# Low parts of split weights by an accumulating transfer: a two-layer hybrid encoder on one core

## The chip, the cores and the metric

One core of a Trainium2 chip runs the kernel. The metric is the device time of one execution in microseconds (us). The engines are TensorE (PE in the profile; its weight loads are PEld), VectorE (DVE), ScalarE (ACT), GpSimd (POOL), and SyncE (SP), which here issues all transfers.

## The reference

Two layers, each on 512 tokens of 1024 channels: an RMS norm modulated by a conditioning vector, one large input projection `w_in`, three branches, and an output projection.

```python
for l in range(DEPTH):
    mod = c_act @ w_ada[l] + b_ada[l]
    shift, scale, gate = jnp.split(mod, 3, axis=-1)
    h = rms_norm(x, norm_w[l]) * (1.0 + scale[:, None, :]) + shift[:, None, :]
    proj = h @ w_in[l]
    ya = mixer_a(qa, ka, va, ...) * jax.nn.silu(ga)
    yb = mixer_b(qb, kb, vb, ...) * jax.nn.silu(gb)
    yc = mixer_c(xc, zc, bc, cc, dtf, dtb, ...)
    g_a, g_b, g_c = jnp.split(jax.nn.sigmoid(mg + b_gate[l]), N_BRANCH, axis=-1)
    merged = (g_a * (ya @ w_proj_a[l]) + g_b * (yb @ w_proj_b[l])
              + g_c * (yc @ w_proj_c[l]))
    x = x + gate[:, None, :] * (merged @ w_out[l])
```

Branch A is grouped-query attention, branch B banded attention at three dilations, branch C a state-space scan in both directions. All of it is in float32.

## The kernel before

**Split matmuls.** TensorE is given its operands as float32r, a rounded float32. Each operand is therefore written as a high part (the value rounded to float32r) and a low part (what the rounding lost), and a product is the sum of three matmuls: high weight by high activation, high weight by low activation, low weight by high activation.

**Chunks.** The weights are stored as 84 chunks per layer of 128 x 1024 numbers (512 KB), each with eight blocks of 128 x 128. `chunk` (line 478) makes one ready: SP loads it into a tile `wraw`, ACT copies it into `whi` with the rounding, and DVE subtracts: `wlo = wraw - whi`. `mm` (line 500) then runs over the blocks k, and for each block `mm_k` (line 490) issues the three matmuls, 24 per chunk, all into one PSUM bank. `proj` (line 510) does this for one 128-channel piece of the input projection; `branch_steps` (line 1217) for the projections of the branches; `out` (line 1247) for the output projection. `v_pair` (line 818) has its own order of the three products. At the start of a layer a few chunks use tiles named `u4` instead of `whi` and `wlo` and are multiplied by `mm_k` directly (lines 1299 to 1303 and 1318 to 1333). Of the 168 chunks, 158 use the tag `wlo`.

**Slots.** Every tile belongs to a tag, and a tag has a fixed number of slots (`SLOTS`, line 408): three each of `wraw`, `whi` and `wlo`. Tiles of 32 conditioning weights (`ada`, line 637) also use `wraw`, and the first sixteen use `whi` and `wlo`.

**Order.** Nothing is issued as written. `Rec.record` (line 199) notes each operation with its cost by a model (a transfer costs its issuing queue 520 or 650 ns, and its bytes divided by a rate on the transfer engines), and `Rec.schedule` (line 277) plans all of them: whichever engine is free takes the ready operation with the lowest priority number for which slots are free. A chunk's preparation is moved ahead of its place by `AHEAD` = 1114 operations (line 415). The plan fixes the order on each engine's queue; on the chip each queue runs in that order and waits where it must. For some operations the plan chooses the engine (`either` and `any2`): the scaling of probabilities and the products and masks of mixer C go to DVE, POOL or ACT.

**Stages of a layer.** Mixer A, mixer B with the projections of branch A, mixer C with those of branch B, then branch C and the output projection. In mixer C, `ssd_head` (line 1162) runs scans on DVE (tiles `P`), multiplies them on POOL or DVE into `u` tiles, ACT copies the high part of each, POOL or DVE makes the low part, and PE multiplies them into `ps_pv`. Gates and projections of other branches fill PE meanwhile.

In the profile nearly all instructions have line 404, where the planned operations are issued, so rows are told apart by their tiles.

Of the kernel before, what the change touches and what calls it, by code (L numbers as in the profile page):

```python
# [7 lines left out]
F32 = mybir.dt.float32  # L8
F32R = mybir.dt.float32r
I32 = mybir.dt.int32  # L10
AF = mybir.ActivationFunctionType
ALU = mybir.AluOpType
# [119 lines left out]
def cost_pe(name, kw, args):  # L132
    if name == "transpose":
        return max(56, 0.417 * args[1].p * 2 + 2, 0.83 * args[1].n)
    l, r = kw["lhsT"], kw["rhs"]
    if r.dt == F32:
        return 2 * max(0.833 * r.n + 2, 0.833 * l.n, 25)
    return max(0.417 * r.n + 2.5, 0.833 * l.n, 25)


def cost_dve(name, out, ins, ptr, n):
    ps = any(v.t.psum for v in ins) or out.t.psum
    if name == "reciprocal":
        return 69 + 6.25 * n
    if name == "tensor_tensor_scan":
        return 69 + SCAN * n
    if name == "memset":
        return 40 + 0.5 * n
    two = len([v for v in ins if v.n and v.n > 1 and v.n >= n]) > 1
    if not two and not ps and name != "tensor_reduce":  # L150
        return 69 + 0.52 * n + 61 * ptr
    return 69 + 1.042 * n + 61 * ptr


def cost_act(name, out, ins, ptr, acc, n):
    return (52 if ins and ins[0].t.psum else 94) + 0.833 * n + 93 * bool(ptr) + 93 * acc


def cost_pool(name, out, ins, ptr, n):
    if name in ("tensor_scalar",):  # L160
        return 245 + 0.83 * n
    if name == "memset":
        return 100 + 0.4 * n
    return 148 + (2.1 if all(v.n == n and not v.wide for v in ins) else 1.67) * n
# [15 lines left out]
class Rec:  # L180
# [18 lines left out]
    def record(self, alts):  # L199
        op = Op()  # L200
        op.i = len(self.ops)
        op.prio = op.i + self.boost
        op.alts = {}
        op.dma = 0
        op.urgent = self.urgent and alts[0][1] != "dma_start"
        for eng, meth, args, kw in alts:
            kw = dict(kw)
            if meth == "matmul":
                kw["lhsT"], kw["rhs"] = args[1], args[2]
            out = kw.get("out", args[0] if args else None)  # L210
            writes = [out] if isinstance(out, V) else []
            if isinstance(kw.get("accum_out"), V):
                writes.append(kw["accum_out"])
            reads = [a for a in args[1:] if isinstance(a, V)] + \
                    [v for k, v in kw.items() if isinstance(v, V) and k not in ("out", "accum_out")]
            n = out.n if isinstance(out, V) else 1
            ptr = sum(1 for v in reads if v.n == 1 and n > 1)
            if meth == "dma_start":
                v = out if isinstance(out, V) else reads[0]
                op.dma = v.n * v.p * 4  # L220
                c = 520
            elif eng == "tensor":
                c = cost_pe(meth, kw, args)
            elif eng == "vector":
                if meth == "tensor_reduce":
                    n = reads[0].n
                c = cost_dve(meth, out, reads, ptr, n)
            elif eng == "scalar":
                c = cost_act(meth, out, reads, ptr, "accum_out" in kw, n)
            else:  # L230
                c = cost_pool(meth, out, reads, ptr, n)
            if meth == "matmul":
                kw.pop("lhsT"), kw.pop("rhs")
            op.alts[ENG[eng]] = (c, eng, meth, args, kw)
        deps = {}
        pe = eng == "tensor"
        for v in reads:
            for o, box, w in v.t.log:
                if w and self.meet(box, v.box):
                    deps[o] = LAT  # L240
        for v in writes:
            if pe and v.t.psum and v.t.lastpe is not None:
                deps.setdefault(v.t.lastpe, 0)
            for o, box, w in v.t.log:
                if o is not op and self.meet(box, v.box) and not (pe and "PE" in o.alts):
                    deps[o] = LAT
        for v in writes:
            if pe and v.t.psum:
                v.t.lastpe = op
            v.t.log = [e for e in v.t.log if not self.inside(e[1], v.box)] + [(op, v.box, True)]  # L250
        for v in reads:
            v.t.log.append((op, v.box, False))
        op.tiles = list({id(v.t): v.t for v in reads + writes}.values())
        for t in op.tiles:
            if t.left == 0:
                t.seq = len(self.tags.setdefault(t.tag, []))
                self.tags[t.tag].append(t)
            t.left += 1
        deps.pop(op, None)
        if meth == "dma_start" and self.hold is not None:  # L260
            deps.setdefault(self.hold, -2000)
        if op.dma and self.hold is not None:
            op.alts = {e: (650,) + a[1:] for e, a in op.alts.items()}
        op.deps = deps
        op.succ = []
        self.ops.append(op)
        return op
# [137 lines left out]


class Kernel:
    SLOTS = {"wraw": 3, "whi": 3, "wlo": 3, "h": 16, "xs": 7, "gate": 3, "merged": 8, "tmp": 6, "P": 3, "bias": 1, "u4": 12, "q": 4, "s1": 32, "sm": 8, "dt": 2, "wa": 1}
    RESERVE = {"u4": 5, "tmp": 2, "sm": 3, "s1": 9, "ps_mm": 0, "ps_tp": 0, "wraw": 0, "q": 1, "ps_pv": 3}
    BYTES = {"wraw": 4096, "whi": 4096, "wlo": 4096, "u4": 4096, "P": 3072, "bias": 10240, "s1": 32, "sm": 256, "dt": 256,  # L410
             "dtr": 256, "dt96": 384}
# [13 lines left out]
    def __init__(self, nc, tc, A, depth=DEPTH, dbg=None):  # L425
        self.real_nc, self.tc, self.A, self.depth, self.dbg = nc, tc, A, depth, dbg or {}
        slots = dict(self.SLOTS)
        slots.update({"ps_" + k: n for k, n in self.BANKS.items()})
# [49 lines left out]
    def chunk(self, l, j, tags=("wraw", "whi", "wlo"), ahead=None, pool=False):  # L478
        nc = self.nc
        b, self.rec.boost = self.rec.boost, self.rec.boost - (self.AHEAD if ahead is None else ahead)  # L480
        raw = self.t(tags[0], [128, 1024])
        nc.sync.dma_start(raw, self.A["wch"][l, j])
        hi = self.t(tags[1], [128, 1024], F32R)
        nc.scalar.copy(hi, raw)
        lo = self.t(tags[2], [128, 1024], F32R)
        self.sub(lo, raw, hi.bitcast(F32), pool)
        self.rec.boost = b
        return hi, lo

# [8 lines left out]
        nc.tensor.matmul(ps, lo[:, c], xh, start=False, stop=(k == nk - 1), **kw)  # L498

    def mm(self, ps, w, c0, nk, xs):  # L500
        for k in range(nk):
            self.mm_k(ps, w, c0, k, nk, xs)

    def soon(self, f):

# [1006 lines left out]
```

## Time and profile before

| | |
|---|---|
| median of 3 runs | 1316.05 us (1314.54 to 1318.47) |
| profiled execution | 1322.19 us |
| its span, first to last instruction | 1320.4 us |
| mean granted TensorE clock | 0.991 |
| instructions | 17528 |
| moved by DMA | 144.30 MB |

The span is what rows and shares of the trace refer to; 1.8 us of the execution lie around it. Busy time of an engine doesn't count issuing and waiting. A wait in a row is idle time of an engine just before an instruction, named with what ended it. Matmuls overlap, so the busy time of a matmul is longer than its distance to the next.

### The profile page before, as it was taken

The page shows a single profiled execution, that of the slowest core. Times are in us where ns is not written, and L with a number is a line of the kernel's source. Part 1 is how long each engine was busy: PE and PEld are TensorE (multiplying, and loading weights), DVE is VectorE, ACT ScalarE, POOL GpSimd, SP SyncE. Part 2 cuts the span into 40 slices and gives each one's busy share as a digit, 9 for nine tenths or more (in the row PEclk, how much of TensorE's full clock was granted, in tenths as well). Part 3 has the DMA queues.
Part 4 walks back from the last instruction along what each step waited for, and adds up shares of the span by engine and source line. Part 5 has one row for each costly group of instructions (what it writes and reads, how often), then busy time and mean ns, then how long its engine had stood idle before and what let it go on. Part 6 is the DMA issues. An engine that isn't in the chain of part 4 may idle for free.

```text
span 1320.4 us, 17528 instructions
## 1 busy us (share of the span) xinstructions
PE 1234.5 (93%) x6240; PEld 1002.4 (76%) x6240; DVE 1040.2 (79%) x1798; ACT 667.4 (51%) x1132; POOL 373.3 (28%) x322
## 2 busy tenths in 40 slices
PE   4899999989999888999999999999998988989998
PEld 1678888778777667778888788887876866767887
DVE  7979975978799989974675999476598998998642
ACT  4447764666555445333334477556565443543330
POOL 3321220011035759610111222100002268583100
PEclk9999999999999999999999999999999999999999
DMA  7644214545322222234632421253342221222441
GB/s 283 237 122 121 69 47 154 187 140 178 108 59 78 64 64 64 66 110 144 222 129 63 130 96 50 79 183 89 95 132 56 81 64 55 73 64 80 136 137 63
DMA packets 49429, 144.30 MB, mean 109 GB/s; under 512 B 7350, under 2 KB 10038, under 8 KB 49342
## 3 DMA queue, kind: packets, MB, share of 16 engines
q1 hardware_dynamic: 49342, 143.19, 34.9%
q8 instruction: 49, 0.80, 0.3%
q14 instruction: 38, 0.31, 0.1%
HBM read 124.74 MB, written 4.27 MB: 98 GB/s over the span
## 4 chain that ended last, share of the span: by engine, by line
PE 63%; DVE 19%; POOL 7%; ACT 4%; issue 3%; DMA 3%; SPq 1%; DVEq 0%; POOLq 0%; ACTq 0%
PE ps_mm L404 47%; PE ps_sc L404 6%; PE ps_tp L404 6%; PE ps_pv L404 5%; DVE P L404 3%; DVE u L404 3%; POOL u L404 3%; DVE wlo L404 3%; DVE xs L404 2%; POOL P L404 1%; DVE q L404 1%; ACT u L404 1%; POOL bias L404 1%; DVE tmp L404 1%; ACT tmp L404 1%
## 5 line engine op out<-in xcount | busy, mean ns | idle before, releaser
L404 PE MATMUL ps_mm<-h,whi 128*128 128x512 f32 x1840 | 601.4, 397 | 1.8 <-ACT gate L404 1.5
L404 PEld LDWEIGHTS ps_mm<-h,whi 128*128 128x128 f32 x1840 | 345.3, 190 | 77.9 <-ACT gate L404 4.8
L404 PE MATMUL ps_mm<-h,wlo 128*128 128x512 f32 x920 | 364.6, 396 | 0.0
L404 DVE TENSOR_TENSOR wlo<-wraw,whi 128x1024 fp32r<-128x1024 f32 x158 | 208.4, 1321 | 84.6 <-ACT whi L404 83.2
L404 ACT CAST whi<-wraw 128x1024 fp32r<-128x1024 f32 x158 | 165.6, 1049 | 179.6 <-PE ps_mm L404 161.1
L404 PEld LDWEIGHTS ps_mm<-h,wlo 128*128 128x128 f32 x920 | 174.4, 190 | 34.7
L404 PE MATMUL ps_mm<-u,whi 128*128 128x512 f32 (+1 forms) x592 | 172.7, 374 | 0.0
L404 POOL TENSOR_SCALAR P<-P,s 128x512 f32<-128x512 f32 (+1 forms) x63 | 54.9, 873 | 339.3 <-DVE s L404 236.0
L404 PE MATMUL ps_pv<-u,u 128*128 128x256 f32 (+2 forms) x640 | 107.0, 293 | 28.4 <-ACT u L404 15.0
L404 PEld LDWEIGHTS ps_mm<-u,whi 128*128 128x128 f32 x592 | 107.7, 188 | 20.0 <-DVE gate L404 0.6
L404 PEld LDWEIGHTS ps_pv<-u,u 128*128 128x128 f32 (+1 forms) x640 | 81.3, 173 | 48.8 <-ACT u L404 21.2
L404 PE MATMUL ps_mm<-u,wlo 128*128 128x512 f32 (+1 forms) x296 | 110.0, 373 | 0.0
L404 ACT CAST u<-ps_tp 128x512 fp32r<-128x512 f32 (+2 forms) x174 | 71.8, 428 | 57.0 <-PE ps_tp L404 47.6
L404 DVE TENSOR_TENSOR_SCAN P<-ps_sc,bias 128x128 f32<-128x128 f32 (+3 forms) x128 | 98.7, 803 | 0.1
L404 DVE TENSOR_TENSOR u<-ps_tp,u 128x512 fp32r<-128x512 f32 (+2 forms) x174 | 81.9, 487 | 19.6 <-ACT u L404 18.9
L404 PE MATMUL ps_sc<-u,q 128*128 128x256 f32 (+1 forms) x320 | 85.9, 365 | 5.5 <-DMA u<-u 3.5
L404 POOL TENSOR_TENSOR tmp<-tmp,tmp 128x512 fp32r<-128x512 f32 (+1 forms) x22 | 32.4, 1474 | 180.4 <-ACT tmp L404 177.4
L404 POOL TENSOR_TENSOR u<-P,u 128x384 f32<-128x384 f32 (+3 forms) x68 | 69.3, 1030 | 15.0 <-DVE P L404 11.4
L404 PE MATMUL ps_tp<-const,P 128*128 128x128 f32 x448 | 67.6, 273 | 5.6 <-DVE s L404 2.3
L404 PEld LDWEIGHTS ps_tp<-const,P 128*128 128x128 f32 x448 | 53.7, 140 | 19.8 <-issue 7.2
L404 PEld LDWEIGHTS ps_sc<-u,q 128*128 128x128 f32 x320 | 52.9, 191 | 19.8 <-issue 6.5
L404 POOL TENSOR_TENSOR u<-u,u 128x1024 fp32r<-128x1024 f32 x24 | 62.3, 2595 | 12.8 <-ACT u L404 12.8
(163 smaller groups left out, 1892.0 us busy)
## 6 DMA issues: line engine op xcount, KB each, us to landing
wraw<-in_wch SPq DMA_DIRECT2D x168, 512.0 KB, 3.6
wraw<-in_wada SPq DMA_DIRECT2D x32, 512.0 KB, 3.8
u<-u SPq DMA_DIRECT2D x28, 256.0 KB, 3.2
merged<-in_xT SPq DMA_DIRECT2D x16, 256.0 KB, 3.2
whi<-in_wada SPq DMA_DIRECT2D x8, 512.0 KB, 4.9
wlo<-in_wada SPq DMA_DIRECT2D x8, 512.0 KB, 9.0
u<-u SPq DMA_DIRECT2D x64, 64.0 KB, 2.6
tmp<-xs SPq DMA_DIRECT2D x40, 64.0 KB, 2.1
```

What stands on the lines that cost most here:

```text
L404: getattr(getattr(nc, eng), meth)(*[get(a) for a in args], **{k: get(v) for k, v in kw.items()})
```

## The change

For chunks with the tag `wlo`, ACT now makes two copies of the raw tile. The first is negated, into `wlo`, so it holds minus the high part. POOL then issues a transfer that reads the same chunk from HBM a second time and adds it to `wlo`. The second copy makes `whi` as before. DVE takes no part. `mm` runs all sixteen matmuls with high weights of a chunk first and then the eight with low weights. `wraw` has two slots instead of three, `wlo` four instead of three. The planner counts an accumulating transfer as twice the bytes, and 1000 ns of the issuing queue for one that POOL issues.

```diff
-                op.dma = v.n * v.p * 4
-                c = 520
+                op.dma = v.n * v.p * (8 if "accum_op" in kw else 4)
+                c = 520 if eng == "sync" else 1000
...
-        if op.dma and self.hold is not None:
+        if op.dma and self.hold is not None and eng == "sync":
             op.alts = {e: (650,) + a[1:] for e, a in op.alts.items()}
...
-    SLOTS = {"wraw": 3, "whi": 3, "wlo": 3, "h": 16, ...
+    SLOTS = {"wraw": 2, "whi": 3, "wlo": 4, "h": 16, ...
...
         hi = self.t(tags[1], [128, 1024], F32R)
-        nc.scalar.copy(hi, raw)
         lo = self.t(tags[2], [128, 1024], F32R)
-        self.sub(lo, raw, hi.bitcast(F32), pool)
+        if tags[2] == "wlo":
+
+            nc.scalar.activation(lo, raw, AF.Copy, scale=-1.0)
+            nc.gpsimd.dma_start(lo, self.A["wch"][l, j], accum_op=ALU.add)
+            nc.scalar.copy(hi, raw)
+        else:
+            nc.scalar.copy(hi, raw)
+            self.sub(lo, raw, hi.bitcast(F32), pool)
...
     def mm(self, ps, w, c0, nk, xs):
+
+        nc = self.nc
+        hi, lo = w
+        c = [slice(c0 + k * 128, c0 + k * 128 + 128) for k in range(nk)]
         for k in range(nk):
-            self.mm_k(ps, w, c0, k, nk, xs)
+            for z, x in enumerate(xs(k)):
+                nc.tensor.matmul(ps, hi[:, c[k]], x, start=(k == 0 and z == 0), stop=False)
+        for k in range(nk):
+            nc.tensor.matmul(ps, lo[:, c[k]], xs(k)[0], start=False, stop=(k == nk - 1))
```

## Rows read from the trace of the kernel before

**Rows 1.** The page, part 1: busy us, share of the span, instructions.

```profile
PE 1234.5 (93%) x6240; PEld 1002.4 (76%) x6240; DVE 1040.2 (79%) x1798; ACT 667.4 (51%) x1132; POOL 373.3 (28%) x322
```

**Rows 2.** The page, part 4: chain that ended last, by engine, by line.

```profile
PE 63%; DVE 19%; POOL 7%; ACT 4%; issue 3%; DMA 3%; SPq 1%; DVEq 0%; POOLq 0%; ACTq 0%
PE ps_mm L404 47%; PE ps_sc L404 6%; PE ps_tp L404 6%; PE ps_pv L404 5%; DVE P L404 3%; DVE u L404 3%; POOL u L404 3%; DVE wlo L404 3%; DVE xs L404 2%; POOL P L404 1%; DVE q L404 1%; ACT u L404 1%; POOL bias L404 1%; DVE tmp L404 1%; ACT tmp L404 1%
```

**Rows 3.** Windows by stretch: us, busy by engine (x instructions), clock, DMA share, GB/s.

```profile
...
400.00:580.00 180.00, 161.93 (x684) 126.26 (x683) 163.27 (x209) 81.87 (x129) 112.41 (x95) 0.98 0.23 71
580.00:675.00 95.00, 95.00 (x504) 81.90 (x503) 59.20 (x96) 34.01 (x50) 10.37 (x8) 1.00 0.47 148
...
1040.00:1220.00 180.00, 162.91 (x695) 127.22 (x694) 165.18 (x213) 83.15 (x130) 111.50 (x95) 0.99 0.23 70
1220.00:1320.40 100.40, 97.05 (x452) 80.83 (x450) 45.50 (x55) 26.56 (x33) 3.87 (x2) 1.00 0.34 110
sum 1240.40, PE 1177.32 PEld 965.15 DVE 976.22 ACT 627.18 POOL 347.93; mean PE 107.03 PEld 87.74 DVE 88.75 ACT 57.02 POOL 31.63
```

**Rows 4.** Waits of PE from 80 us on: us in total, times, longest.

```profile
PE ps_pv L404 <- ACT u L404: 15.0, 12, 3.9
PE ps_pv L404 <- POOL u L404: 8.8, 8, 2.5
```

**Rows 5.** Timeline, 552 to 566 us, of DVE, POOL and PE: start, us, instruction.

```profile
554.70 5.30 DVE L404 TENSOR_TENSOR wlo<-wraw,whi 128x1024 fp32r<-128x1024 f32 x2
...
555.55 3.36 POOL L404 TENSOR_TENSOR u<-u,u 128x1024 fp32r<-128x1024 f32 x1
561.79 1.27 POOL L404 TENSOR_TENSOR u<-P,u 128x512 f32<-128x512 f32 x1 [2.88 <-DVE P L404]
...
564.19 0.60 PE L404 MATMUL ps_pv<-u,u 128*128 128x512 f32 x1 [1.89 <-ACT u L404]
```

**Rows 6.** The page, part 5: groups; busy us, mean ns, idle before.

```profile
L404 DVE TENSOR_TENSOR wlo<-wraw,whi 128x1024 fp32r<-128x1024 f32 x158 | 208.4, 1321 | 84.6 <-ACT whi L404 83.2
L404 ACT CAST whi<-wraw 128x1024 fp32r<-128x1024 f32 x158 | 165.6, 1049 | 179.6 <-PE ps_mm L404 161.1
```

**Rows 7.** Waits of DVE: us in total, times, longest.

```profile
DVE wlo L404 <- ACT whi L404: 83.2, 47, 8.1
```

**Rows 8.** Windows of the instructions on `wlo` alone, columns as in rows 3.

```profile
400.00:580.00 180.00, 73.63 (x186) 35.49 (x186) 35.02 (x24) 0.00 (x0) 0.00 (x0) 0.98 0.23 71
580.00:675.00 95.00, 48.98 (x133) 25.06 (x133) 15.88 (x13) 0.00 (x0) 0.00 (x0) 1.00 0.47 148
1220.00:1320.40 100.40, 56.41 (x150) 28.03 (x149) 18.91 (x16) 0.00 (x0) 0.00 (x0) 1.00 0.34 110
```

**Rows 9.** Groups by form on POOL, 400 to 600 us.

```profile
L404 POOL TENSOR_TENSOR u<-u,u 128x1024 fp32r<-128x1024 f32 x12 | 31.1, 2594 | 6.4 <-ACT u L404 6.4
```

**Rows 10.** Instructions on `wraw`: durations in ns, min/median/max.

```profile
L404 SPq DMA_DIRECT2D wraw<-in_wch x168: 327/328/761, 10.3 to 1286.3; - x168
```

**Rows 11.** DMA: the queue; loads at the start; landings on `wraw`.

```profile
q1 hardware_dynamic: 49342, 143.19, 34.9%
...
wlo<-in_wada SPq DMA_DIRECT2D x8, 512.0 KB, 9.0
...
DMA to landing us min/median/max: 3.3/3.6/7.8
```

**Rows 12.** One window of 40 us in the dense stretch, columns as in rows 3.

```profile
600.00:640.00 40.00, 40.00 (x178) 33.13 (x177) 21.41 (x25) 15.75 (x20) 0.00 (x0) 1.00 0.45 142
```

**Rows 13.** Timeline, 604 to 612 us, of ACT and DVE.

```profile
605.23 1.05 ACT L404 CAST whi<-wraw 128x1024 fp32r<-128x1024 f32 x1 [3.12 <-PE ps_mm L404]
...
608.93 0.69 DVE L404 TENSOR_TENSOR merged<-merged,gate 128x512 f32<-128x512 f32 x1
...
610.31 0.69 DVE L404 TENSOR_TENSOR u<-merged,u 128x512 fp32r<-128x512 f32 x1 [0.69 <-ACT u L404]
```

More of the change, by code (lines that the diff above doesn't have):

```diff
@@ L407 @@
 class Kernel:
-    SLOTS = {"wraw": 3, "whi": 3, "wlo": 3, "h": 16, "xs": 7, "gate": 3, "merged": 8, "tmp": 6, "P": 3, "bias": 1, "u4": 12, "q": 4, "s1": 32, "sm": 8, "dt": 2, "wa": 1}
+    SLOTS = {"wraw": 2, "whi": 3, "wlo": 4, "h": 16, "xs": 7, "gate": 3, "merged": 8, "tmp": 6, "P": 3, "bias": 1, "u4": 12, "q": 4, "s1": 32, "sm": 8, "dt": 2, "wa": 1}
     RESERVE = {"u4": 5, "tmp": 2, "sm": 3, "s1": 9, "ps_mm": 0, "ps_tp": 0, "wraw": 0, "q": 1, "ps_pv": 3}
```

## The prediction

> **What bounds the kernel now.** I begin with busy time [rows 1]: TensorE 1234.5 us of 1320.4 (93%), VectorE 1040.2 (79%), ScalarE 667.4, GpSimd 373.3. TensorE is the bound, and the question is how much of the span it isn't working. The chain that ended last [rows 2] gives 63% to PE but 19% to DVE and 7% to POOL, and 3% (some 40 us) to the subtraction `wlo` itself, the instruction that the change takes away. The table by stretch [rows 3] shows where. In 580 to 675 us PE is busy 95.00 of 95.00: branch C and the output projection, with nothing to win. From 80 us on PE is busy 1177.3 of 1240.4, so it idles 63 us. The two stretches with the scans of mixer C, 400 to 580 and 1040 to 1220, have 18.1 + 17.1 = 35 us of that, and there DVE is busy 163.3 and 165.2 of 180 (91%) and POOL 112. Idle time in the first 80 us stays: its chunks have low parts under another tag, which the change leaves alone.
>
> Who ends PE's waits [rows 4]: on the mixers' `u` tiles ACT 15.0 us and POOL 8.8. These are the last links of a chain that begins on DVE, and one place shows it [rows 5]. At 554.70 two `wlo` subtractions hold DVE for 5.30 us, twice what two means of 1.32 us [rows 6] would take, while POOL works on its own `u` from 555.55 to 558.91. The scan queued behind them comes late, POOL idles 2.88 us for it, and PE 1.89 us for ACT, which copies what POOL made. The mean granted clock of the two stretches is 0.98 and 0.99 [rows 3]; between the levels of 2.4 and 1.2 GHz, 0.98 is 4% of the time at the lower one and 2% of it lost.
>
> **The change part by part.** *Removed from DVE:* 158 subtractions of 1321 ns, 208 us [rows 6], and 83.2 us in which DVE stood at one waiting for ACT's high copy [rows 7]. In 400 to 580 it is 24 of them, 35.0 us [rows 8], so DVE falls there from 163 to about 128 us of 180. DVE then stops being full, and PE's idle time is the bound on the gain: 35 us, and by the clock 2% and 1% of 180 us, 5 more. The gaps could also stay, as latencies of ACT and POOL, so the ends are 0 and 40. I take half, 20 us: a gap like that of [rows 5] goes, but a wait whose last link is POOL's own product of 2.6 us [rows 9] stays. Outside these stretches PE idles 63 − 35 = 28 us; DVE is only one of several releasers there, so of 0 to 28 I take 8.
>
> *Added to ACT:* 158 negated copies 128x1024. The trace has the same shape without a scale, 1049 ns [rows 6]: 166 us, and ACT goes from 51% to 63%. It is hidden wherever ACT isn't what PE waits for. If that cover is gone, a copy out of PSUM stands behind one more copy of 1.05 us: with the 20 waits of PE on ACT or POOL [rows 4], the ends are 0 and 21 us. At 13% more busy time, half a copy each, they come to 1.4 us; I take 4, since waits that are short now count too.
>
> *Added to POOL:* 158 issues of transfers. POOL issues none now. From below: SP's issue, 0.33 us [rows 10]; from above: a whole POOL instruction on 128x1024, 2.6 us [rows 9]. I take 1 us, nearer the issue since no element passes through POOL. That is 24 us on the 112 of 180 in mixer C, covered by 68 us of idle time. Behind an issue that waits for ACT's negated copy everything on POOL waits too (products and masks of the scans), and PE through ACT, as in [rows 5]. I add 4 us for that.
>
> *Added to the DMA engines:* 158 x 0.524 MB more from HBM, with the old content read as well. The one queue moves 143.19 MB in 34.9% of 16 engines' span [rows 11]: 460.8 us / 143.19 = 3.22 us per MB, 1.69 us per chunk. No row has an accumulating transfer; it costs between a plain one and several of them. I take twice, 3.4 us, for two reads. 158 of them are 40% of the span, beside 35% in use. In the dense stretch 580 to 675, with 0.47 in use [rows 3] and 13 subtractions [rows 8], it makes 0.47 + 13 x 3.4 / 95 = 0.93. Just hidden.
>
> The Trainium skill (Collectives: The Full Stack, Part 3, on why ReduceScatter is half of AllGather) says that an add in the transfer is paid as a second read on the same ring, so an estimate by that page is twice a copy. By it the sum is the one made here; at a plain copy's price the same stretch would stand at 0.70, and no term would change. No row of this trace can say which holds.
>
> *Latency of a low part:* copy 1.05, issue 1, landing. A chunk lands in 3.6 us, at worst 9.0 like the loads that crowd the start [rows 11]; so 6 to 11 us. Dense matmuls take 40 us / 178 = 0.225 us each [rows 12], a chunk of 24 takes 5.4. With four `wlo` slots the negated copy can begin when the chunk four before has ended, and with the high passes first the low part is wanted 16 x 0.225 = 3.6 us into its own chunk: 3 x 5.4 + 3.6 = 20 us of cover. No price.
>
> *`wraw` from 3 to 2 slots:* in the dense stretch a high copy starts when PE frees its `whi` slot (605.23, after an idle 3.12 us [rows 13]), so now the raw data lies ready early. Two slots give 2 x 5.4 = 10.8 us per load; it needs issue 0.33, landing 3.6, two copies 2.1 and some hand-overs, 6.3. No price; it would be one with landings over 8 us (7.8 is the longest now [rows 11]). SP issues the same transfers as before; behind a load that waits for a slot, the moves `u<-u` and `tmp<-xs` wait, and PE for them.
>
> *High passes first:* same matmuls and weight loads. PE frees `whi` 8 x 0.225 = 1.8 us sooner. It wants the last high part of the moving operand after 14 instead of 21 matmuls; where that is fresh, at the output projection, addition, copy and subtraction run from 608.93 to 611.00 [rows 13], 2.1 us under 14 x 0.225 = 3.2. Nothing.
>
> **Sum.** −20 − 8 + 4 + 4 = −20 us on the profiled execution of 1322.2 us (span 1320.4): 1302. The median of the runs shown is 1316.05, 6 us less: **1296 us**.
>
> **Rivals.** *POOL takes DVE's place (slower).* An issue is dear, or stands waiting for ACT in front of POOL's scan products. In mixer C POOL has 180 − 112 = 68 us left for 24 issues [rows 3, 8]: it decides from 2.8 us each, waits included. At 3.3 us POOL needs 112 + 79 = 191, 11 us over per stretch. Then the 20 us are not won and 22 are lost: 1296 + 42 = 1338. For: the nearest POOL row above is 2.6 us, and DVE stood 83 us at this very hand-over from ACT [rows 7]. Against: the negated copy has a slot more than the high copy had, so it waits less for PE.
>
> The Trainium skill (SBUF — State Buffer, under its two separate sides, the trap that DVE blocks DMA) adds that descriptors of transfers issued from POOL are written by software, which stands still while DVE runs an instruction that takes both its ports. That would lengthen an issue by the rest of such an instruction; no run so far shows it.
>
> *The DMA engines become the bound (slower).* At three times a copy, 5.1 us, the dense stretches overflow: 0.47 x 95 + 13 x 5.1 = 111 of 95, and in 1220 to 1320, with 0.34 in use and 16 subtractions [rows 3, 8], 34 + 82 = 116 of 100. It decides from (95 − 45) / 13 = 3.9 us each. The two cost 16 + 16 = 32 us: 1328, and late loads into two raw slots would come on top. For: no row excludes that price. Against: DMA is in use only 35% of the span.
>
> *Given back (no change).* Several operations may go to DVE or POOL, and the planner, charging POOL 1 us an issue, moves POOL's products to the emptied DVE; PE's gaps end by ACT as before. Only the 8 us outside mixer C remain, less the 8 added: 1316.
>
> *More than forecast.* All of mixer C's 40 us and half of the 28, less 8 added: 1316 − 46 = 1270.
>
> That the change doesn't do what it says is no rival with a price: the two new lines fix the added work.
>
> **How the numbers follow.** A measurement of this kernel can tell about 0.3%, 4 us, from no change. Forecast and its larger case 0.54; given back 0.13; POOL 0.15; DMA 0.11; ACT's extra copies ahead of copies out of PSUM (21 us and nothing won, 1337) 0.07. Faster 0.54, same 0.13, slower 0.33. The likeliest one's own range is 1270 to 1312; reaching to POOL's and DMA's prices, 1266 to 1342 leaves out a dearer transfer or issue.
>
> **What would show it.** Right: DVE near 830 us busy, ACT near 833; in mixer C shorter waits of PE on ACT `u` and POOL `u`, and DVE under 75%; no PE wait on `wlo` in 580 to 675. Wrong: POOL over 90% in mixer C; PE waiting for the transfers into `wlo`, or high copies waiting for `wraw`; a DMA share near 1 in dense stretches; landings of raw chunks over 8 us.

## The result, and the profile after

The kernel after the change takes 1336.63 us (median of 4 runs, 1334.81 to 1339.14); the kernel before, on the same chip, 1317.26. The ratio is 1.0148 (95% interval 1.0119 to 1.0177): slower by some 19 us. The forecast was 1296 us, faster; the time lies inside its range, on the other side.

The page of the kernel after, cut to the rows that answer to [rows 1], [rows 2], [rows 6] and [rows 11]: busy time by engine, the DMA queues, the chain, two groups, the DMA issues with their median landing.

```profile
PE 1241.8 (93%) x6240; PEld 1006.2 (75%) x6240; DVE 877.2 (66%) x1712; ACT 821.7 (61%) x1288; POOL 412.9 (31%) x410
...
q0 software_dynamic: 22752, 82.85, 36.6%
q1 hardware_dynamic: 49342, 143.19, 33.1%
...
PE 28%; DVE 10%; DMA 3%; issue 3%; ACT 2%; POOL 0%; SPq 0%; ACTq 0%; DVEq 0%; POOLq 0%
...
L404 POOL DMA_DIRECT2D wlo<-in_wch x158 | 138.0, 873 | 617.9 <-ACT wlo L404 582.0
...
L404 ACT ACTIVATE wlo<-wraw 128x1024 fp32r<-128x1024 f32 x158 | 167.3, 1059 | 75.7 <-PE ps_mm L404 38.4
...
wraw<-in_wch SPq DMA_DIRECT2D x168, 512.0 KB, 4.4
wlo<-in_wch POOLq DMA_DIRECT2D x158, 512.0 KB, 6.1
...
u<-u SPq DMA_DIRECT2D x28, 256.0 KB, 6.5
```

Against [rows 1], DVE lost 163 us of work and ACT gained 154, as intended; PE has the same 6240 matmuls. The chain adds up to under half of the span: it broke off on its way back, so it is no help here, and windows must do. Of the 16.9 us by which the profiled span grew (1320.4 to 1337.3), PE's idle time is 9.6 (85.9 to 95.5); the other 7.3 are the same matmuls keeping PE busy for longer, at a mean granted clock of 0.982 instead of 0.991.

The last three rows are the surprise. The accumulating transfer lands in 6.1 us, and transfers that the change doesn't touch became slow: a raw chunk 4.4 instead of 3.6 [rows 11], a 256 KB move `u<-u` 6.5 instead of 3.2. These moves copy keys of mixers A and B from one half of a tile's partitions to the other; 6.5 is the median of the 9 of 28 whose landing the trace tells, 3.2 that of 10. From the kernel before, the moves and PE's wait for them:

```profile
u<-u SPq DMA_DIRECT2D x28, 256.0 KB, 3.2
```

```profile
PE ps_sc L404 <- DMA u<-u: 3.5, 8, 0.8
```

Windows of the kernel before: mixer B of layer 0, then mixer C of both layers from its first scan to its last (us, busy by engine in the order PE, PEld, DVE, ACT, POOL, then clock, DMA share, GB/s).

```profile
251.80:372.10 120.30, 113.89 (x664) 93.05 (x665) 97.85 (x238) 73.55 (x129) 13.67 (x12) 0.99 0.47 143
404.20:560.90 156.70, 140.51 (x593) 108.98 (x592) 148.49 (x182) 72.78 (x115) 109.86 (x93) 0.99 0.21 64
1044.80:1203.20 158.40, 143.19 (x606) 111.18 (x605) 150.24 (x185) 73.07 (x116) 108.95 (x93) 0.99 0.22 67
```

The same stages of the kernel after, and the dense stretch of [rows 3]:

```profile
252.50:387.70 135.20, 122.03 (x691) 98.43 (x691) 88.67 (x239) 90.50 (x149) 30.35 (x30) 0.97 0.81 203
415.50:562.50 147.00, 134.71 (x558) 103.73 (x556) 133.02 (x188) 87.39 (x127) 90.24 (x86) 0.98 0.61 132
580.00:675.00 95.00, 95.00 (x473) 80.62 (x472) 37.73 (x64) 45.04 (x59) 16.99 (x19) 1.00 0.85 219
1064.90:1210.80 145.90, 133.80 (x566) 104.33 (x564) 131.21 (x186) 90.10 (x134) 85.09 (x82) 0.99 0.62 134
```

A stage's matmuls differ between the plans, so compare idle time (length minus PE), not length. Mixer C: 16.2 + 15.2 us of PE idle became 12.3 + 12.1, a gain of 7. Mixer B of layer 0: 6.4 became 13.2, with the clock at 0.97 and the DMA share up from 0.47 to 0.81. The dense stretch: still 95.00 of 95.00.

PE's waits in the kernel after, from 80 us on (us in total, times, longest), against [rows 4]:

```profile
PE ps_tp L404 <- DVE u L404: 8.2, 11, 1.9
...
PE ps_pv L404 <- ACT u L404: 6.7, 8, 1.7
...
PE ps_mm L404 <- DMA wlo<-in_wch: 5.9, 3, 3.4
...
PE ps_mm L404 <- ACT whi L404: 4.9, 2, 4.1
PE ps_sc L404 <- DMA u<-u: 3.9, 6, 1.2
...
PE ps_pv L404 <- POOL u L404: 0.3, 1, 0.3
```

The waits that were to shrink did: 15.0 to 6.7 on ACT, 8.8 to 0.3 on POOL. New ones stand beside them, for low parts that had not landed and for high copies that came late. The largest one, on DVE's `u`, was 0.9 before. Two of the new ones can be followed. The timeline of the kernel after at mixer B of layer 1 (start, us, instruction; chosen rows of PE, ACT, POOL and SP, in order of time):

```profile
879.97 1.84 SPq L404 DMA_DIRECT2D wraw<-in_wada  x2
...
886.50 0.33 SPq L404 DMA_DIRECT2D wraw<-in_wch  x1
...
892.45 1.06 ACT L404 ACTIVATE wlo<-wraw 128x1024 fp32r<-128x1024 f32 x1
...
893.80 0.85 POOL L404 DMA_DIRECT2D wlo<-in_wch  x1 [21.84 <-ACT wlo L404]
894.85 2.04 SPq L404 DMA_DIRECT2D u<-u  x3
895.26 3.79 PE L404 MATMUL ps_mm<-h,whi 128*128 128x512 f32 x16
902.42 3.68 PE L404 MATMUL ps_mm<-h,wlo 128*128 128x512 f32 x8 [3.37 <-DMA wlo<-in_wch]
```

Two `wada` chunks took both `wraw` slots at 879.97; the raw `wch` chunk could be issued at 886.50 and was negated at 892.45. POOL, idle for 21.84 us, issued when the negated copy was there; the transfer, among `u<-u` moves, took 8.6 us (893.80 to 902.42; the three landings here are 8.6 to 10.6). The high passes covered 3.8 us. Then PE pays twice: in the window behind the wait its granted clock is 0.58.

```profile
895.00:902.40 7.40, 4.04 (x18) 3.00 (x16) 5.82 (x7) 4.08 (x5) 0.86 (x1) 1.00 0.95 210
902.40:906.50 4.10, 4.08 (x11) 3.22 (x12) 0.00 (x0) 2.35 (x3) 0.86 (x1) 0.58 1.08 264
906.50:915.00 8.50, 8.50 (x42) 6.84 (x41) 2.40 (x6) 5.22 (x8) 1.82 (x2) 1.00 1.04 245
```

11 matmuls took 4.1 us, 0.37 each, against 0.20 in the next window: the lower of the levels 1.2 and 2.4 GHz for most of it, after an engine that had idled. The DMA share is 0.95 to 1.08 in these windows.

The wait for a high copy, mixer B of layer 0 (chosen rows of DVE, SP, ACT and PE):

```profile
317.88 2.12 SPq L404 DMA_DIRECT2D wraw<-in_wada  x2
324.88 1.21 DVE L404 SCALAR_TENSOR_TENSOR wraw<-wraw,const 128x1024 f32<-128x1024 f32 x1
326.13 0.33 SPq L404 DMA_DIRECT2D wraw<-in_wch  x1
331.28 1.06 ACT L404 ACTIVATE wlo<-wraw 128x1024 fp32r<-128x1024 f32 x1
332.24 1.03 ACT L404 CAST whi<-wraw 128x1024 fp32r<-128x1024 f32 x1
333.32 6.71 PE L404 MATMUL ps_mm<-h,whi 128*128 128x512 f32 x16 [4.12 <-ACT whi L404]
```

The two `wraw` slots had taken two `wada` chunks, which DVE reduces itself. Only when DVE had read one could SP load the next `wch` chunk, 326.13; ACT then makes the negated copy first and the high copy second, and PE, which needs only the high one, starts at 333.32. In the window behind the wait the granted clock is again low (0.55):

```profile
333.30:340.00 6.70, 6.68 (x16) 4.99 (x16) 6.07 (x8) 2.99 (x4) 1.08 (x2) 0.55 0.93 205
```

### The profile page after: what moved, and what is told of

Same layout as the page of the kernel before. It is cut to its first block, busy times and chain, and to the rows that moved or that the text cites. A ratio compares the mean times of both kernels' runs of the same rounds, so it can differ in the third digit from the quotient of the medians.

```text
span 1337.3 us, 17687 instructions
## 1 busy us (share of the span) xinstructions
PE 1241.8 (93%) x6240; PEld 1006.2 (75%) x6240; DVE 877.2 (66%) x1712; ACT 821.7 (61%) x1288; POOL 412.9 (31%) x410
## 3 DMA queue, kind: packets, MB, share of 16 engines
q0 software_dynamic: 22752, 82.85, 36.6%
## 5 line engine op out<-in xcount | busy, mean ns | idle before, releaser
L404 PE MATMUL ps_mm<-h,whi 128*128 128x512 f32 x1840 | 488.3, 399 | 11.4 <-ACT gate L404 5.5
L404 POOL DMA_DIRECT2D wlo<-in_wch x158 | 138.0, 873 | 617.9 <-ACT wlo L404 582.0
L404 PE MATMUL ps_mm<-h,wlo 128*128 128x512 f32 x920 | 253.9, 401 | 5.9 <-DMA wlo<-in_wch 5.9
L404 ACT ACTIVATE wlo<-wraw 128x1024 fp32r<-128x1024 f32 x158 | 167.3, 1059 | 75.7 <-PE ps_mm L404 38.4
L404 PE MATMUL ps_mm<-u,whi 128*128 128x512 f32 (+1 forms) x592 | 140.6, 375 | 0.0
L404 DVE SCALAR_TENSOR_TENSOR gate<-gate,ps_mm 128x512 f32<-128x512 f32 x52 | 35.4, 681 | 91.6 <-PE ps_mm L404 69.6
L404 PE MATMUL ps_sc<-u,q 128*128 128x256 f32 (+1 forms) x320 | 82.8, 360 | 4.1 <-DMA u<-u 3.9
L404 DVE TENSOR_TENSOR tmp<-tmp,tmp 128x512 fp32r<-128x512 f32 (+1 forms) x25 | 20.3, 813 | 90.6 <-ACT tmp L404 90.4
L404 PE MATMUL ps_mm<-u,wlo 128*128 128x512 f32 (+1 forms) x296 | 75.0, 374 | 0.0
```

The costliest lines, as they stand in the source:

```text
L404: getattr(getattr(nc, eng), meth)(*[get(a) for a in args], **{k: get(v) for k, v in kw.items()})
```

## The experiments

Ratios are to the kernel before, with 95% intervals; 1% is 13 us. Except where said, the planner makes a new order of work for each kernel, which is itself a cause of differences; so two runs touch only a planner constant.

**What freeing DVE is worth, and what comes between.** `e12_nosub` keeps the order and slots of before and leaves out the 158 subtractions. `e13_nodma` is the kernel after, its plan kept, with no transfer issued.

```diff
+            if o.i in self.skip:            # e12: when the plan is emitted
+                lo, hi = self.skip[o.i]
+                lo.t.real = hi.t.real
+                continue
...
+            if "accum_op" in kw:            # e13: when the plan is emitted
+                continue
```

> The kernel before in its own plan with the 158 subtractions left out and nothing in their place; the low passes read the high tile, so matmuls are the same in number and size and the output is not the reference's. My prediction's gain for freeing DVE was 28 us: then 1285 to 1298. If PE's gaps are latencies of other engines and the plan's order keeps the rest: 1306 to 1318.

> The changed kernel in its own plan with the accumulating transfers not issued at all (wlo stays minus the high part, not the reference's output): no traffic, no landing, no issue on POOL. If POOL's 158 issues and their waits for ACT cost something of their own: 5 us or more faster than the eighth-size transfer's 1317.6. If not: within 4 us of it.

Measured: `e12_nosub` 1285.49 us, 0.9748 (0.9731 to 0.9765). `e13_nodma` 1307.19 us, 0.992 (0.9904 to 0.9936). First the two mixer C windows of `e12_nosub`, then mixer B of layer 0 in `e13_nodma`:

```profile
401.30:542.20 140.90, 133.16 (x568) 106.00 (x567) 119.25 (x162) 71.81 (x115) 95.37 (x92) 0.98 0.22 68
1023.60:1164.90 141.30, 133.45 (x577) 106.36 (x576) 120.33 (x162) 71.57 (x116) 94.97 (x92) 0.99 0.23 72
```

```profile
248.90:378.40 129.50, 120.95 (x692) 99.14 (x691) 88.92 (x239) 90.80 (x149) 16.68 (x14) 0.97 0.47 140
```

A free DVE is worth 33 us, and mixer C's idle time falls from 31.4 to 15.6. So the goal was real. With the same plan and no transfer, PE idles 8.6 us in mixer B instead of 13.2; its 4.1 us wait for the high copy stays, so no transfer makes it. PE's total wait on DVE's `u` is 5.6 us there, so most of the 8.2 isn't the transfers' either.

**The transfer, cut into its costs.** Both runs have the plan of the kernel after, as `e13_nodma` has. `e3_eighth` accumulates 64 KB of each chunk instead of 512. `e11_nowait` moves as many bytes the other way, from `wlo` added into a scratch in HBM, so PE doesn't wait for the landing.

```diff
-            nc.gpsimd.dma_start(lo, self.A["wch"][l, j], accum_op=ALU.add)
+            nc.gpsimd.dma_start(lo.custom(lambda t: t[:, 0:128]), self.A["wch"][l, j][:, 0:128], accum_op=ALU.add)   # e3
...
+            if "accum_op" in kw:                                                                # e11, when the plan is emitted
+                self.nst += 1
+                nc.gpsimd.dma_start(self.scratch[self.nst % 16].real(), args[0].real().bitcast(F32), accum_op=ALU.add)
+                continue
```

> The changed kernel in the very same plan and order, but each accumulating transfer moves 128 of the 1024 columns (64 KB instead of 512 KB); the low parts of the other columns stay minus the high part, so the output is not the reference's. If the traffic of the second reading is the cause (DMA share 0.70 instead of 0.35, moves u<-u landing in 6.5 instead of 3.2 us): 12 to 20 us faster than the changed kernel, so within 6 us of before or better, and the landings back near 3.2. If the plan, ACT's copies or the two raw slots are the cause: within 5 us of the changed kernel's 1337.

> The changed kernel in its own plan, each accumulating transfer with the same bytes, issue and wait for the negated copy, but added from wlo into a scratch area in HBM: PE's low passes don't wait for its landing (wlo stays minus the high part; the output is not the reference's). If the landing in front of the low passes is what costs the 20 us against the eighth-size transfer: 1313 to 1322. If it is the traffic, in the way of u<-u and the raw loads: 1330 to 1345.

Measured: `e3_eighth` 1317.58 us, 0.999 (0.9977 to 1.0003); `e11_nowait` 1329.17 us, 1.0082 (1.0061 to 1.0103). The issues and landings of `e3_eighth`, then of `e11_nowait` with PE's wait for the moves:

```profile
wraw<-in_wch SPq DMA_DIRECT2D x168, 512.0 KB, 3.6
...
wlo<-in_wch POOLq DMA_DIRECT2D x158, 64.0 KB, 2.7
u<-u SPq DMA_DIRECT2D x28, 256.0 KB, 3.2
```

```profile
q0 software_dynamic: 22752, 82.85, 37.9%
...
wraw<-in_wch SPq DMA_DIRECT2D x168, 512.0 KB, 4.3
dram<-wlo POOLq DMA_DIRECT2D x158, 512.0 KB, 5.8
...
u<-u SPq DMA_DIRECT2D x28, 256.0 KB, 6.1
```

```profile
PE ps_sc L408 <- DMA u<-u: 6.3, 8, 1.5
```

With an eighth of the bytes, the raw chunks and the 256 KB moves land as before, and the whole change costs nothing; with all the bytes and PE not waiting for their landing, the moves `u<-u` stay at 6.1 us, and the time lies just under the second of the two expected ranges. From `e13_nodma` the steps are: issues and short landings 0.7%, 9 us; traffic 0.9%, 12 us; waiting for the landing 0.7%, 9 us (this one between transfers of opposite direction). Together 30.

Since these kernels have one plan, the same matmul can be found in every trace, and each step has a place. Lengths in us, profiled executions, both layers together:

| matmuls of 6240 | `e13_nodma` | `e3_eighth` | `e11_nowait` | after |
|---|---|---|---|---|
| mixer B: 961 to 1800, 4081 to 4920 | 304.4 | 305.3 | 314.8 | 322.0 |
| mixer C: 1921 to 2520, 5161 to 5760 | 311.0 | 316.2 | 320.2 | 318.8 |
| all others | 688.8 | 690.8 | 692.6 | 696.5 |

The issues with their short landings cost most in mixer C (5.2 of 8.1 us), traffic and landings in mixer B (9.5 of 15.3, then 7.2 of 9.7). In mixer B PE waits for the moves for 0 us with an eighth of the bytes and for 6.1 with all of them (3.7 + 2.4, of the 6.3 above); mixer C's 4.0 us under traffic go with PE busy for longer, at a granted clock of 0.98 and 0.97 instead of 1.00.

**The order and the slots alone.** `e1_order` is before with the high passes first; `e2_slots` before with two `wraw` and four `wlo` slots; `e14_orderslots` has both, with DVE subtracting. `e5_inplace` keeps the plan of before and only reorders PE's passes within their places.

```diff
-    SLOTS = {"wraw": 3, "whi": 3, "wlo": 3, ...     # the line is cut
+    SLOTS = {"wraw": 2, "whi": 3, "wlo": 4, ...     # e2, e14
...
+        g = [self.mm_k(ps, w, c0, k, nk, xs) for k in range(nk)]                       # e5
+        self.groups.append([o for t in g for o in t[:2]] + [t[2] for t in g])
```

> The kernel before, with the high passes of a chunk first in mm and nothing else of the change. If the new order of passes (and the plan that follows from it) is what costs time: 10 to 20 us slower than before. If the cause is the second reading of the weights, the two raw slots or ACT's extra copies: within 4 us of before.

> The kernel before, with wraw in two slots and wlo in four; DVE still subtracts. If two raw slots hold the loads back (ACT waited 36.8 us for raw chunks in the changed kernel, 2.2 before): 8 us or more slower, with ACT or DVE waiting for DMA wraw. If traffic or the order is the cause: within 4 us.

> The kernel before with the change's order of passes and its slots (wraw 2, wlo 4), and DVE subtracting as before. Each alone cost 1.0 to 1.2%. If they add up: 1340 to 1350, and the accumulating transfer then gained some 10 us in the change. If they overlap: 1330 to 1337, the time of the changed kernel, and the mechanism itself is worth nothing there.

> The kernel before in its own plan; after planning, the matmuls of a chunk are put into the order high passes first within the places that they have on TensorE's queue, nothing else moves. The new order alone, planned anew, cost 1.2%. If the order itself costs that (the last high part wanted sooner, whi freed sooner): again 10 us or more slower. If it was the new plan that cost it: within 4 us of before.

Measured: `e1_order` 1334.87 us, 1.0122 (1.0093 to 1.0151); `e2_slots` 1332.86, 1.0099 (1.0075 to 1.0123); `e14_orderslots` 1334.42, 1.0123 (1.0099 to 1.0147); `e5_inplace` 1322.05, 1.0032 (1.0017 to 1.0048). Mixer C of layer 0 in `e1_order`:

```profile
404.80:571.00 166.20, 147.09 (x612) 112.93 (x611) 161.59 (x195) 74.66 (x117) 108.82 (x87) 0.98 0.22 67
```

Both edits that were priced at nothing cost 1% each, not added up when together. The order itself costs 0.3%; the rest of its 1.2% comes with the new plan, which puts 13 us more of DVE work into mixer C of layer 0 (161.59 against 148.49), the stage in which `e12_nosub` shows that DVE is in PE's way. With the new slots alone, ACT waits 12.5 us for raw chunks instead of 2.2; whether that makes the 1%, or again the new plan, isn't shown.

**How much a plan scatters.** `n1_lat` changes the planner's latency constant, `n2_margin` its margin.

```diff
-LAT = 200
+LAT = 205          # n1_lat
...
-    margin = 200
+    margin = 210    # n2_margin
```

> The kernel before with a planner's constant touched (LAT, the latency between engines, 205 instead of 200): the same work, another plan. If a new plan is as good as the old: within 4 us of before. If the old plan is a lucky one, and any new plan costs what the order or the slots alone did: 8 to 18 us slower.

> The kernel before with another planner's constant touched (margin, 210 instead of 200): a second plan of the same work, to see how far plans scatter. Same two expectations: within 4 us, or 8 to 18 us slower.

Measured: 1322.13 us, 1.0021 (1.0005 to 1.0036), and 1324.26 us, 1.0045 (1.0029 to 1.0061). So a plan that is only different costs up to about 0.45%; both touches made it slower, the second to between its two expectations. The 1.2% is more than either, but two touches are a small sample, and why the planner does worse with the high passes first isn't settled.

**The mechanism without order, without slots, without both.** The kernel after with one or both undone, each planned anew.

```diff
         for k in range(nk):                             # e6, e10: mm as before
-            for z, x in enumerate(xs(k)):
-                nc.tensor.matmul(ps, hi[:, c[k]], x, start=(k == 0 and z == 0), stop=False)
...
+            self.mm_k(ps, w, c0, k, nk, xs)
...
-    SLOTS = {"wraw": 2, "whi": 3, "wlo": 4, ...     # e8, e10; the line is cut
+    SLOTS = {"wraw": 3, "whi": 3, "wlo": 3, ...
```

> The changed kernel with the old order of passes (high, high, low for each block), planned anew. If the costs add up, the order being 1.2% and the traffic the rest: 1318 to 1326. If high passes first are what hides the late low parts (landing 6.1 us after an issue): PE waits for DMA wlo in many places and it is slower than the changed kernel, over 1345.

> The changed kernel with three slots each of wraw, whi and wlo as before. If the two raw slots cost it 1% as they cost the kernel before: 1320 to 1328. If the fourth wlo slot is needed to hide the transfer: slower than the changed kernel, over 1342.

> The changed kernel with the old order and the old slots, so the mechanism alone (negated copy, accumulating transfer), planned with its costs. If order and slots are costs that add up and freeing DVE gains about 25 us: 1305 to 1318. If order and slots are what makes the mechanism bearable: over 1345.

Measured: `e6_oldmm` (old order) 1353.93 us, 1.0277 (1.0236 to 1.0319); `e8_slots3` (old slots) 1370.34, 1.0405 (1.0367 to 1.0443); `e10_both` 1397.35, 1.0599 (1.0571 to 1.0627). PE's waits in `e10_both` from 80 us on:

```profile
PE ps_mm L404 <- ACT gate L404: 25.7, 16, 3.2
PE ps_mm L404 <- DMA wlo<-in_wch: 16.2, 10, 3.0
```

PE's waits for landings go from 5.9 us to 16.2 without the fourth slot and the high passes first, and its waits on ACT's gates from 5.5 to 25.7. So the two edits cost 16 us in the kernel before and save 59 under the transfers (5.99% against 1.48%); what makes up all of the 59 isn't shown. The moves `u<-u` land in 4.1 us here, with the same 83 MB: how much they suffer depends on what the plan puts beside them.

**Transfers that the plan doesn't know.** `e7_sameplan` puts the negated copy and the transfer where the plan of before has the subtraction, with its slots and the in-place order of `e5_inplace`. `e4_store` keeps everything of before, and POOL issues a plain store of each low part.

```diff
+                nc.scalar.activation(lo.real(), raw.real(), AF.Copy, scale=-1.0)     # e7
+                nc.gpsimd.dma_start(lo.real(), src, accum_op=ALU.add)
...
+            if meth == "tensor_sub" and args[0].t.tag == "wlo":                          # e4, behind each subtraction
+                self.nst = getattr(self, "nst", -1) + 1
+                nc.gpsimd.dma_start(self.scratch[self.nst % 16].real().bitcast(F32), args[0].real().bitcast(F32))
```

> The same, and in the places of the 158 subtractions of that plan the negated copy on ACT and the accumulating transfer from POOL; slots 3/3/3 as before, DVE's places stay empty. So the change's mechanism without a new plan. If the second reading's traffic is what costs 19 us: 1335 to 1350, as the freed DVE gives little. If the new plan and slots cost the time and the mechanism gains: 1290 to 1312. If POOL's queue is the trouble where the plan doesn't know of the issues: over 1355, with mixer C longer by 10 us or more in each layer.

> The kernel before, its plan unchanged, with a plain 512 KB store of every finished wlo to a scratch area in HBM, issued by POOL: traffic and POOL's issues of the change without its ACT copies, its order or its slots. If traffic and POOL's issues cost the time: 8 to 25 us slower than before, above all in the stretch of mixer B. If not: within 4 us of before.

Measured: `e7_sameplan` 1417.4 us, 1.0756 (1.0727 to 1.0784); `e4_store` 1378.78 us, 1.0454 (1.0421 to 1.0486). PE's costliest wait in `e7_sameplan`; then the page and PE's costliest waits of `e4_store`:

```profile
PE ps_sc L410 <- DMA u<-u: 28.2, 9, 6.4
```

```profile
q0 software_dynamic: 22752, 82.85, 14.8%
...
u<-u SPq DMA_DIRECT2D x28, 256.0 KB, 3.6
```

```profile
PE ps_pv L404 <- ACT u L404: 23.9, 13, 4.0
PE ps_pv L404 <- POOL u L404: 18.6, 13, 3.3
```

In `e7_sameplan` the moves come too late for PE (28.2 us against 3.5 in the kernel before), and its waits on ACT and POOL grow from [rows 4] to 23.6 and 15.8. `e4_store` carries as many bytes at less than half the engine time (14.8% of the span against 36.6%), and its 256 KB moves land in 3.6 us. It loses some 60 us all the same, more than either expectation allowed. PE's waits on POOL and ACT grow most, from [rows 4] to 18.6 and 23.9: there an issue waits for DVE's subtraction in front of POOL's products. Its waits for the moves grow too, from 3.5 to 10.2. The first of these is the first rival, in a kernel whose planner doesn't see the issue; in the changed one, which plans it, the waits on POOL and ACT shrank.

**Other ways to free DVE.** `e9_conly` takes the negated copy and transfer only for chunks recorded in mixer C, with old order and slots. `e15_pool` lets the planner put the subtraction on DVE or POOL; `e16_poolside` does so only outside mixer C.

```diff
+        if tags[2] == "wlo" and self.acc_on:                                       # e9, acc_on in mixer C alone
...
-        self.sub(lo, raw, hi.bitcast(F32), pool)
+        self.sub(lo, raw, hi.bitcast(F32), pool or tags[2] == "wlo")               # e15
```

> Old order and slots, and the accumulating transfer for the chunks of mixer C alone, where DVE was 91% busy and DMA in use 23%; elsewhere DVE subtracts. If the loss is traffic where transfers are on the path (mixer B, its moves u<-u), and the gain is DVE's in mixer C: 1300 to 1315, mixer C shorter by 5 to 10 us a layer. If the mechanism gains nothing in mixer C either: 1317 to 1330.

> The kernel before, with the planner free to put each subtraction on DVE or POOL (one POOL instruction of 128x1024 takes 2.6 us, DVE's 1.3). If any relief of DVE pays that adds no transfer: 1300 to 1314. If POOL, already 62% busy in mixer C, gets in the way of its own products there: 1318 to 1330.

> The same, but chunks recorded in mixer C stay with DVE, so POOL is only asked where it was 15% busy. If POOL's own work in mixer C is the obstacle to e15, this is the faster of the two, 1305 to 1316. If the gain of a freed DVE lies in mixer C alone (20 of the 33 us in the kernel without subtractions): within 4 us of before.

Measured: `e9_conly` 1343.62 us, 1.0186 (1.0169 to 1.0203); `e15_pool` 1373.1, 1.0408 (1.0381 to 1.0435); `e16_poolside` 1341.34, 1.0169 (1.014 to 1.0197). None beats the kernel before, and all three are slower than either of their expectations allowed; why isn't shown. `e9_conly` has 52 of the 158 transfers, where the DMA engines were least in use, and loses all the same: PE waits 5.4 us for landings in it and 8.0 for the moves. With its old order and slots it doesn't show what such a choice would be worth under the new ones. Where low parts could come from without DVE, POOL or a transfer wasn't tried.

## Why the prediction was wrong

The runs can be put in a row from before to after, in per cent of 1317 us. Order and slots +1.2% (`e14_orderslots`). Negated copies for subtractions, no transfer, −2.0% (to `e13_nodma`, with a new plan). Issues and short landings +0.7%, traffic +0.9%, waiting for the landing +0.7%. Sum +1.5%: some 16 − 27 + 9 + 12 + 9 = 19 us.

These are differences between neighbours, so they add up by construction, and another row gives other shares: by `e10_both` the mechanism costs 6.0% and order and slots give back 4.5%. On the row here, the gain came near its size: −27 for DVE and ACT together, where −24 was said. What failed are the terms set at nothing, traffic, landing, and slots and order, which cost 12, 9 and 16 us; the issues cost 9 for 4. That the time lies inside the stated range is luck: its upper end stood for POOL becoming full in mixer C or the DMA engines in the dense stretches, and neither did (61% and 0.85).

**DVE freed: right.** The terms were −20 and −8; `e12_nosub` shows −33. In mixer C PE's idle time fell by 15.8 us there, for the 20; the kernel after got only 7 of them. DVE was to be at 830 us and under 75% of mixer C; it is at 877 and 90% (133.02 of 147.00). The planner gave DVE products that POOL had, as the rival "Given back" said (POOL has 70 instructions fewer besides the issues, DVE 72 more besides the subtractions): POOL's work without the issues is 412.9 − 138.0 = 275 us, 98 less than in [rows 1].

**ACT's copies: right within what is known.** Predicted +4. From `e14_orderslots` to `e13_nodma` 27 of the 33 us of `e12_nosub` are left, which would leave some 6 for the copies; over two plans that is no bound. In the same step PE's waits on ACT's gates and high copies grow by 6.4 us (2.3 + 1.7 to 5.5 + 4.9). ACT is at 822 us, 833 was said.

**POOL's issues: mis-sized.** 1 us each was near (0.87, 853 to 1025 ns on all 158), and POOL did not become full: 90.24 of 147.00 us in mixer C. But issue and a short landing cost 9 us, not 4, most of it in mixer C, where the prediction looked for it.

The Trainium skill (SBUF — State Buffer, two separate sides, the trap that DVE blocks DMA) would have the descriptors of such transfers held up while DVE runs an instruction in a two-port mode. At the issue this trace shows nothing of it: with DVE busy for 66% of the span, the slowest of 158 took 1025 ns. Whether the transfer's own start was held up isn't shown.

**DMA traffic, "Just hidden": the step that failed.** The price per byte was close: 36.6% of 1337.3 us for 82.85 MB is 5.9 us of 16 engines per MB, 1.8 times the plain 3.22 of [rows 11], where twice was taken. The place was wrong. Cover was worked out where PE is densest, and there the sum held: 0.93 forecast, 0.85 measured, PE 95.00 of 95.00. But in that stretch PE waited for no transfer. In mixer B it waits for what the moves `u<-u` carry, 6.1 us in `e11_nowait` against 0 in `e3_eighth`, and there the share went from 0.47 to 0.81 on average and to 0.95 or more from 895 to 915. That is about half of the 12 us. The DMA rival had the right resource in the wrong stage: it was to decide from 3.9 us a chunk, and 3.1 (5.9 x 0.524) were enough.

The Trainium skill (Collectives: The Full Stack, Part 3) counts an add as a second read; the 1.8 agrees with it nearly. A right price per byte did not save the sum.

**Latency of a low part, "No price": failed.** It was 20 us of cover against 6 to 11. Landing alone is 6.1 at the median and 12.4 at the longest; and for the low part that PE had at 902.42 the cover was 5 us, from the issue at 893.80 to 899.05, when PE wanted it. Its raw chunk was issued only at 886.50, so ACT negated it at 892.45, in the very chunk before its use, not as soon as a `wlo` slot was free. Slots bound how early a low part can begin, not how early it does. Price 9 us, 7.2 of the profiled 9.7 in mixer B.

**`wraw` from 3 to 2 slots, "No price", and high passes first, "Nothing": failed.** `e2_slots` 1.0%, `e1_order` 1.2%. The dense stretch was the ground for the slots as well: 10.8 us per load for 6.3 needed. In mixer B the slots are shared with `wada` chunks that DVE frees, and the wait at 333.32 stands behind one; this wait alone was followed, and what makes the rest of `e2_slots`'s 1% stays open. For the order, the matmuls really cost next to nothing (0.3%); what was left out is that the edit goes through a planner that then makes another order for everything.

So the mechanism of the gain was right; three costs (traffic, landing, slots) that were covered in the stretch where cover is largest were not covered elsewhere, and the fourth, the order, came with a new plan. The chance of slower, 0.33, stood for POOL, the dense stretch and ACT; none of the three brought it as it was told, though POOL's issues cost twice their term.

## What to carry to other kernels

Ask of each stage, before adding transfers: is a transfer on its path? There the new one can be paid in the latency of the others before the engines are full on average (0.81 in mixer B here), and a cover worked out where the matmuls are dense says nothing about it. Measure the ceiling of a change by leaving out what it removes (here 2.5%), and its price by leaving out what it adds. Where a planner makes the order of work, a reordering or a slot costs what its new plan costs: touch a constant to see the scatter first.

## What the runs showed of the hardware

- An accumulating transfer of 512 KB from HBM, issued by POOL, lands in 6.1 us (4.7 to 12.4), where a plain load had 3.6 in the kernel before and 4.4 beside it. In engine time per byte it is 1.8 times a plain load, and a plain store from SBUF (`e4_store`: 14.8% of 1374.3 us, 2.5 us per MB) is cheaper than both.
- A 256 KB move within SBUF goes from 3.2 to 6.5 us with 83 MB more of accumulating traffic beside it, and back to 3.2 with an eighth of that (medians of the 9 or 10 landings of 28 that the traces tell). In another plan with the same traffic it is 4.1 (`e10_both`). Under `e4_store`'s plain stores, as many bytes, it lands in 3.6.
- Behind the two waits of PE followed above, 3.4 and 4.1 us long, come 4.1 and 6.7 us at a mean granted clock of 0.58 and 0.55; over the kernel the mean fell from 0.991 to 0.982, and the same matmuls kept PE busy for 7.3 us more.
